# One gather for eight experts, nine whole units, and the overflow branch behind the output

## The chip, the cores and the metric

The kernel runs on one core of one Trainium2 chip. The time is that of the device for one execution, in microseconds. TensorE is PE, with its weight loads as PEld; VectorE is DVE, ScalarE is ACT, GpSimd is POOL, and SyncE (SP) issues nearly all of the DMAs. Three executions of the kernel before took 1276.86, 1276.93 and 1277.24 us; the median is 1276.93.

## The reference

Two transformer blocks over 256 tokens of 1024 values, in fp32. The first has a gated mixer of three branches and a feed-forward layer; it isn't touched. The second has two kinds of attention and, at its end, a layer of 32 experts, to which nearly all of the change belongs:

```python
h2 = _modulate(_rmsnorm(x, g_ffn), shift_ffn, scale_ffn)
group = argmax(softmax(h2 @ w_group))                     # 1 of 4 groups
top_p, top_local = top_k(softmax(expert logits within the group), 2)
weight = group_gate * top_p / sum(top_p)
y[token] = sum over its two experts e of
           weight * ((silu(h2 @ w_gate[e]) * (h2 @ w_up[e])) @ w_down[e])
x = x + gate_ffn * y
out = _rmsnorm(x, g_final)
```

Each expert has w_gate and w_up (1024x512) and w_down (512x1024): 6 MiB in fp32, 192 MiB for all 32.

## The kernel before

**Units.** All weights come as units of 1 MiB (128 partitions x 2048 values), in the order of a plan: 127 units for what stands ahead of the experts, then 192, six for each expert (two each of `eg`, `eu` and `ed`: gate, up and down). `prefetch` (L295) issues a unit's DMA on SP (L302) as soon as one of 18 buffers (`units`) is free and fewer units than a cap wait unconverted. The `units` buffers also hold the converted weights, the hidden values `gy` and a few others, so that the release of any of them can let a DMA start.

**Conversion.** TensorE multiplies in a reduced form of fp32 (fp32r), so each unit is split: ACT rounds it (`hi<-raw`, L221, where all of ACT's operations are recorded), DVE subtracts (`lo<-raw,hi`, L344), and PE multiplies with both (`pe<-hi,xs`, `pe<-lo,xs`; all of PE's matmuls are recorded at L237). `take_unit` (L350) converts two units ahead of the one in use. A *whole* unit (`whole`, L290) isn't split: PE takes it as plain fp32, one pass over `raw` that needs more time per column (each of its matmuls shows as two records). Counted from the first expert unit, units 9, 25, 41, ..., 185 are whole: twelve.

**Order.** The program runs over pairs of experts, p = 0 to 16. In step p stand gate and up of experts 2p and 2p+1 (`gate_up`), in their middle the hidden layer of pair p-1 (`hidden`: `pT<-cst,gy`, silu, `hsz`), and then the downs of pair p-1 (`down`: `pd`); so 12 units a step. Each expert has 32 token slots. `gather(g)` copies tokens into the slots of four experts, by 32 matmuls with a 0/1 matrix `oh` (`pg`), split into high and low part, and eight copies by ACT into `xs` (two buffers, each for four experts). `put_back` brings the results of eight experts back to the tokens: 32 fp32 matmuls (`py<-ws,gy`, 64 records), then additions to `x` on DVE (L1582). It comes after p=4, 8 and 12, for four pairs each; a put_back of three pairs, 12 to 14, comes after p=15, and one of the last pair at the end. When it is done, its `gy` buffers come free.

Such pieces stand in a list `bg`. `pull` takes one piece of it for each half unit, so gathers and put_backs are strewn between the matmuls of the units; `drain` empties the list at once. `post` sets off a step some half units later, and `flush` does all that are due. `st["order"]` = 1 holds the strewn pieces behind the conversion just issued.

**End.** More tokens may choose an expert than it has slots. How many are left over is summed (`full`, L1635), brought to one value by a matmul (`pn`), and turned into a number (`left`, L1639); every engine loads that (L1640) and passes a branch (`tc.If`, L1641). Behind it is a loop over all experts for the tokens left over; with these inputs there are none. After the branch come the last put_back, the sum of squares (`ss<-sq,ones`), `rstd` and the output, written in place of `x` and sent by four DMAs.

Of the kernel before, what the change touches and what calls it, by code (L numbers as in the profile page):

```python
# [213 lines left out]
def block_kernel(ctx: ExitStack, tc: tile.TileContext, A, out):  # L214
# [21 lines left out]
    def mm(*a, **k):  # L236
        last["mm"] = T.matmul(*a, **k).ins  # L237
# [21 lines left out]
    def ps(name="ps"):  # L259
        return psum.tile([P, 512], F32, name=name, tag="ps")  # L260
# [4 lines left out]
    def t256(name, dt=F32, shape=(P, 256)):  # L265
        return tmp.tile(list(shape), dt, name=name, tag="r", bufs=4)
# [7 lines left out]
    def flat(ap):  # L274
        return ap.rearrange("p k t -> p (k t)")

    def over2(r):
        return bc(r[:, None, :], [P, 2, 256])
# [11 lines left out]
    def whole(u):  # L290

        m = u - MOE0
        return m < NU - MOE0 - 4 and m % 16 == 9

    def prefetch(upto=-1):  # L295
        while st["dma"] < NU and ((len(raw) < st["cap"] and live[0] < NS) or st["dma"] <= upto):
# [99 lines left out]
    def post(fn, n=1):  # L396
        due.append((st["step"] + n, fn))
# [15 lines left out]
    def flush():  # L413
        settle(True)
# [18 lines left out]
    def drain():  # L433
        while bg or bg2:
            pull(1000)
# [67 lines left out]
    def rstd_of(acc, mult=1.0):  # L503
        r = t256("rstd")
        act(r, acc[:, :256], AF.Sqrt, bias=epst, scale=mult)
        V.reciprocal(r, r)  # L506
        return r
# [892 lines left out]
    def weights():  # L1400

        V.tensor_tensor(ge, lg[:, :, 0:4], bc(gv[:, :, None], [P, 2, 4]), op=OP.subtract)
        V.tensor_tensor(ge, ge, bc(rk[:, :, None], [P, 2, 4]), op=OP.mult)
        act(ge, ge, AF.Exp)
        V.tensor_tensor(ed, top[:, 1], top[:, 0], op=OP.subtract)
        V.tensor_tensor(ed, ed, rk, op=OP.mult)
        act(ed, ed, AF.Exp)
        V.tensor_tensor(ms, at, end_slot, op=OP.is_lt)
        V.tensor_tensor(jk, pick, bc(ms[:, None], [P, 2, 2, 32]), op=OP.mult)
        V.tensor_reduce(fit, jk, axis=AX.X, op=OP.add)  # L1410
        V.tensor_reduce(gs, ge, axis=AX.X, op=OP.add)
        V.reciprocal(gs, gs)
        V.tensor_scalar(wt[:, 1], ed, 1.0, None, op0=OP.add)
        V.reciprocal(wt[:, 1], wt[:, 1])
        V.tensor_tensor(wt[:, 0], gs, wt[:, 1], op=OP.mult)
        V.tensor_tensor(wt[:, 1], wt[:, 0], ed, op=OP.mult)
        for q in range(1, 4):
            slg.append(rtile(2, 2))
            V.tensor_scalar(slg[q], sl, -256.0 * q, None, op0=OP.add)


    xg, wsel = {}, {}
# [6 lines left out]
        G.memset(t[:, :, :, 64:128].bitcast(F32), 0.0)  # L1429
    for t in hsz:  # L1430
        G.memset(t[:, :, 64:128].bitcast(F32), 0.0)
    ohs = {}

    def gather(g):

        if g % 2 == 0:
            oh = ohs[g // 2] = [pairs.tile([P, 256], F32R, name="oh", tag="oh", bufs=4) for tt in range(2)]
            for tt in range(2):
                t1 = t256("oh1")
                V.tensor_scalar(t1, slot, slg[g // 2][:, 0, tt:tt + 1], None, op0=OP.is_equal)  # L1440
                last["oh"] = V.scalar_tensor_tensor(oh[tt], slot, slg[g // 2][:, 1, tt:tt + 1], t1,
                                                    op0=OP.is_equal, op1=OP.add).ins
            yield
            yield
        oh = [t[:, (g % 2) * 128:(g % 2 + 1) * 128] for t in ohs[g // 2]]
        for k2 in range(4):
            p = ps("pg")
            for kk in range(2):
                k = 2 * k2 + kk
                for i, h in enumerate((hth, htl)):  # L1450
                    c = slice(kk * 256 + i * 128, kk * 256 + (i + 1) * 128)
                    for tt in range(2):
                        mm(p[:, c], h[:, tt, k * 128:(k + 1) * 128], oh[tt],
                           start=kk + i + tt == 0, stop=tt == 1, skip_group_check=True)

            def keep(k2=k2, p=p):
                pv = p.rearrange("p (k i a b r) -> p k i a b r", k=2, i=2, a=2, b=2)
                for kk in range(2):
                    o = xs[g % 2][:, 2 * k2 + kk].rearrange("p a (h i r) -> p a h i r", h=3, i=2)
                    last["xg"] = act(o[:, :, 0:3:2], pv[:, kk].rearrange("p i a b r -> p a b i r"), AF.Copy)  # L1460
            post(keep, 2)
            yield

    def put_weights(g):
# [61 lines left out]
    def hidden(q):  # L1526

        t = gy[q]
        p = ps("pT")
        for f in range(8):  # L1530
            mm(p[:, f * 64:(f + 1) * 64], t[:, f * 128:(f + 1) * 128], fold, start=True, stop=True)
        sg = t256("sgm")
        hs = hsz[q % 2]
        sv = sg.rearrange("p (f e r) -> p f e r", f=4, e=2)
        ho = hs.rearrange("p f (h i r) -> p f h i r", h=3, i=2)

        def product():
# [12 lines left out]
    def down(e, hs):  # L1550
        odd = e % 2 == 1
        if not odd:
            pds[:] = [ps("pd"), ps("pd")]
        for k2 in range(2):
            for ws in take_unit("ed", e, k2):
                rows_times([(pds[n], window(hs[:, 2 * k2 + i], e), 2 * i + n, not odd and k2 + i == 0,
                             odd and k2 + i == 2) for i in range(2) for n in range(2)])(ws)
        if odd:
            y = gy[e // 2]

            def keep(pd=list(pds)):
                for n in range(2):
                    if n and e == NE - 1:
                        V.tensor_copy(y[:, n * 512:(n + 1) * 512], pd[n])
                    else:
                        act(y[:, n * 512:(n + 1) * 512], pd[n], AF.Copy)
            post(keep, 2)
# [37 lines left out]
    for p in range(NE // 2 + 1):  # L1605
        if p < NE // 2:
            gate_up(2 * p)
        if p:
            if p == NE // 2:
                flush()  # L1610
            hs = hidden(p - 1)
            if p == NE // 2:
                flush()
        if p < NE // 2:
            gate_up(2 * p + 1)
            if p % 2 == 0 and p < NE // 2 - 2:
                bg.append(gather(p // 2 + 1))
            if p % 4 == 2:
                bg.append(put_weights(p // 4))
            if p % 2 == 1:  # L1620
                drain()
        if p:
            for e in (2 * p - 2, 2 * p - 1):
                down(e, hs)
            if p % 4 == 0 and p < NE // 2:
                post(lambda p=p: bg.insert(0, put_back([p - 4, p - 3, p - 2, p - 1])), 3)
            elif p == NE // 2 - 1:
                post(lambda p=p: bg.insert(0, put_back([p - 3, p - 2, p - 1])), 3)
# [2 lines left out]
    flush()  # L1631


    full = tmp.tile([P, 1], F32, name="full", tag="full", bufs=1)
    V.tensor_reduce(full, fit, axis=AX.XY, op=OP.add)  # L1635
    pn = ps("pn")
    mm(pn[:1, :1], full, one1[:, 0:1], start=True, stop=True)
    left = tmp.tile([1, 1], mybir.dt.int32, name="left", tag="left", bufs=1)
    V.tensor_scalar(left, pn[:1, :1], -1.0, 512.0, op0=OP.mult, op1=OP.add)  # L1639
    n_left = nc.values_load(left, min_val=0, max_val=512)  # L1640
    with tc.If(n_left > 0):  # L1641
        hx = k8(unit("hx"))
# [66 lines left out]
                                           op0=OP.mult, op1=OP.add)  # L1709
            free(6)  # L1710
        free(2)


    acc = ps("ss")

    zero = tmp.tile([P, 1], F32, name="zero", tag="full", bufs=1)
    ctx.enter_context(tc.issue_after(act(zero, x[:, 0, 0:1], AF.Sqrt, scale=0.0)))
    V.tensor_add(epst, epst, zero)
    back = []
    for _ in put_back([NE // 2 - 1], back.append):  # L1720
        pass
    end = last["mm"]
    for f2, add in enumerate(back):
        add()
        with tc.issue_after(end):
            square_sum(acc, flat(x[:, 2 * f2:2 * f2 + 2]), f2 == 0, f2 == 3)
    r = rstd_of(acc)
    for k2 in range(4):
        for k in (2 * k2, 2 * k2 + 1):
            act(x[:, k], x[:, k], AF.Copy, scale=vec("g_final_2", k))  # L1730
        x2 = x[:, 2 * k2:2 * k2 + 2]
        (G if k2 == 3 else V).tensor_tensor(x2, x2, over2(r), op=OP.mult)  # L1732
        nc.sync.dma_start(out[:, 2 * k2:2 * k2 + 2], x2)


# [19 lines left out]
```

## Time and profile before

| | us |
|---|---|
| median of three executions | 1276.93 |
| the profiled execution | 1279.84 |
| its span, first to last instruction | 1278.0 |
| PE busy in it | 1204.2 (94%) |
| DVE busy | 1034.0 (81%) |
| ACT busy | 796.7 (62%) |
| mean granted TensorE clock | 0.975 |

The span is what the trace shows; the profiled execution is 1.84 us longer, and 2.9 us above the median. Times in the rows count from the start of the span. The expert part runs from about 740 to 1252 us. HBM reads are 338.88 MB in all.

### The profile page before, as it was taken

Reading aid. Unit: us, or ns where it says so; the run is one execution under the profiler, and the core shown is the slowest. Engines: PE = TensorE matmul, PEld = TensorE weight load, DVE = VectorE, ACT = ScalarE, POOL = GpSimd, SP = SyncE. Lnnn points to the kernel's source line nnn. Section 1 sums busy time; section 2 is a strip of 40 time slices with the busy share of each in tenths; the row PEclk is TensorE's granted clock in tenths of the full one; section 3 lists DMA queues with packets and bytes.
Section 4 is the critical chain, followed back from the end, with each engine's and each line's share of the span. In section 5 each row is a group of like instructions: output and inputs, shape, how many; then the busy total and the mean of one; then the engine's idle time right before and its main releaser. Section 6 shows DMA issues by size and latency. Waiting matters only on the chain. (4 is left out here: it accounts for less than half of the span.)

```text
span 1278.0 us, 19089 instructions
## 1 busy us (share of the span) xinstructions
PE 1204.2 (94%) x7588; PEld 1058.0 (83%) x7588; DVE 1034.0 (81%) x1221; ACT 796.7 (62%) x917; POOL 105.3 (8%) x106
## 2 busy tenths in 40 slices
PE   6987999999999999889999999999999999999984
PEld 6985899999999999888888878777877787778763
DVE  6699999968798889666646778986998699869973
ACT  5576645375654444645465379886888688867852
POOL 2559400210000000000000000000000000000000
PEclk9999999999999999999989989999999999999997
DMA  9732257437887988232127059999899989998941
GB/s 365 283 132 99 100 201 276 150 116 285 333 301 295 343 322 322 108 133 99 67 72 291 1 198 415 421 421 387 336 421 421 400 342 421 422 395 334 421 199 35
DMA packets 48622, 341.22 MB, mean 267 GB/s; under 512 B 5392, under 2 KB 5648, under 8 KB 7824
## 3 DMA queue, kind: packets, MB, share of 16 engines
q1 hardware_dynamic: 47664, 337.65, 66.8%
q10 hardware_dynamic: 864, 2.31, 0.5%
q8 instruction: 61, 1.00, 0.3%
q14 instruction: 33, 0.27, 0.1%
HBM read 338.88 MB, written 1.05 MB: 266 GB/s over the span
## 5 line engine op out<-in xcount | busy, mean ns | idle before, releaser
L221 ACT ACTIVATE hi<-raw 128x1024 fp32r<-128x1024 f32 (+1 forms) x388 | 556.8, 1453 | 299.0 <-issue 47.6
L344 DVE TENSOR_TENSOR lo<-raw,hi 128x2048 fp32r<-128x2048 f32 (+1 forms) x182 | 405.1, 2264 | 67.6 <-ACT hi L221 48.9
L323 DVE TENSOR_TENSOR lo<-raw,hi 128x1024 fp32r<-128x1024 f32 x206 | 259.8, 1268 | 75.9 <-ACT hi L221 72.0
L237 PE MATMUL pe<-lo,xs 128*128 128x512 f32 x480 | 135.0, 406 | 5.9 <-DVE lo L344 5.5
L237 PE MATMUL pe<-hi,xs 128*128 128x512 f32 x480 | 137.3, 410 | 1.2 <-ACT xs L221 1.1
L237 PEld LDWEIGHTS pe<-lo,xs 128*128 128x128 f32 x480 | 87.5, 189 | 34.1 <-DVE lo L344 15.9
L237 PEld LDWEIGHTS pe<-hi,xs 128*128 128x128 f32 x480 | 89.9, 191 | 25.7 <-issue 3.3
L640 DVE SCALAR_TENSOR_TENSOR ca<-ch,par,ca 128x246 f32<-128x246 f32 (+25 forms) x180 | 100.8, 588 | 0.9
L237 PE MATMUL pd<-hi,hsz 128*128 128x512 f32 x240 | 68.0, 405 | 3.0 <-DVE hsz L1543 3.0
L237 PE MATMUL pd<-lo,hsz 128*128 128x512 f32 x240 | 67.0, 401 | 2.0 <-DVE lo L344 1.6
L237 PE MATMUL py<-ws,gy 128*128 128x256 f32 x256 | 60.3, 392 | 5.9 <-PEq L1641 5.5
L237 PEld LDWEIGHTS py<-ws,gy 128*128 128x128 f32 x256 | 50.2, 197 | 14.0 <-issue 5.5
L631 POOL TENSOR_TENSOR ca<-ca,tap 128x255 f32<-128x255 f32 (+29 forms) x60 | 57.9, 966 | 33.2 <-ACT tap L221 29.6
L237 PEld LDWEIGHTS pd<-hi,hsz 128*128 128x128 f32 x240 | 45.1, 188 | 15.9 <-issue 5.3
L314 DVE SCALAR_TENSOR_TENSOR raw<-raw,aux 128x1024 f32<-128x1024 f32 x48 | 56.8, 1220 | 0.0
L237 PEld LDWEIGHTS pd<-lo,hsz 128*128 128x128 f32 x240 | 44.4, 189 | 14.9 <-DVE lo L344 5.1
L237 PE MATMUL pgt<-nh,hi 128*128 128x256 f32 x192 | 54.2, 282 | 0.0
L237 PE MATMUL pgt<-nl,hi 128*128 128x256 f32 x192 | 53.9, 281 | 0.0
L237 PE MATMUL pgt<-nh,lo 128*128 128x256 f32 x192 | 53.7, 280 | 0.0
L237 PE MATMUL pfg<-xh,hi 128*128 128x256 f32 x176 | 49.7, 282 | 0.0
L237 PE MATMUL pfg<-xl,hi 128*128 128x256 f32 x176 | 49.5, 281 | 0.0
L237 PE MATMUL pfg<-xh,lo 128*128 128x256 f32 x176 | 49.5, 281 | 0.0
(349 smaller groups left out, 2954.7 us busy)
## 6 DMA issues: line engine op xcount, KB each, us to landing
raw<-in_ws_dram SPq DMA_DIRECT2D x318, 1024.0 KB, 8.7
x<-in_xt_dram SPq DMA_DIRECT2D x4, 256.0 KB, 4.2
raw<-in_ws_dram SPq DMA_DIRECT2D x2, 512.0 KB, 8.1
out_dram<-x SPq DMA_DIRECT2D x4, 256.0 KB, 2.7
aux<-in_sguw_dram ACTq DMA_DIRECT2D x1, 512.0 KB, 9.6
aux<-in_cnt_dram SPq DMA_DIRECT2D x1, 512.0 KB, 12.7
aux<-in_sgub_dram ACTq DMA_DIRECT2D x1, 512.0 KB, 3.9
aux<-in_cvec_dram ACTq DMA_DIRECT2D x1, 512.0 KB, 4.7
```

Source lines behind the costliest of these rows:

```text
L221: ins = S.activation(out, in_, func, **k).ins
L237: last["mm"] = T.matmul(*a, **k).ins
L314: V.scalar_tensor_tensor(r, r, 1.0, cond["c"], op0=OP.mult, op1=OP.mult, accum_out=mod[:, col:col + 1])
L323: st["lo"] = V.tensor_sub(lo, r, hi).ins
L344: st["lo"] = V.tensor_sub(lo[:, c], raw[u][:, c], hi[:, c]).ins
L631: G.tensor_tensor(ca[:, j, d:], ca[:, j, d:], t[:, :256 - d], op=OP.add)
L640: V.scalar_tensor_tensor(ca[:, j, d:], ch[:, j, :256 - d], w(30 - d), ca[:, j, d:], op0=OP.mult, op1=OP.add)
```

## The change

1. `gather(g)` serves eight experts: 32 matmuls of 256 columns into eight `pg` tiles, and sixteen copies into both `xs` buffers. There are four gathers in place of eight. The first stands ahead of the loop, as before; the others are listed at p=3, 7 and 11 instead of at every second p, behind a `drain`, with two pieces pulled for each half unit (`st["bg"] = 2`), and end with a `drain` behind the downs.
2. `whole` takes every twentieth unit: 9, 29, 49, ..., 169, nine in all. Units 57, 105, 153 and 185 among others are split now.
3. At p=16 the list is emptied ahead of the last hidden layer, and the strewn order is given up (`st["order"] = 0`): the put_back of pairs 12 to 14 is written out there.
4. `full`, `pn` and `left` are computed at the start of the expert part (`weights`).
5. The last put_back, the sum of squares, `rstd` and the output (`finish`, to a new buffer `xo`) stand ahead of the branch, and once more in it, for the case of left tokens.

```diff
-        return m < NU - MOE0 - 4 and m % 16 == 9
+        return m < NU - MOE0 - 4 and m % 20 == 9
...
+        V.tensor_reduce(full, fit, axis=AX.XY, op=OP.add)
+        pn = ps("pn")
+        mm(pn[:1, :1], full, one1[:, 0:1], start=True, stop=True)
+        V.tensor_scalar(left, pn[:1, :1], -1.0, 512.0, op0=OP.mult, op1=OP.add)
...
-        for k2 in range(4):
+        yield
+        for k in range(8):
             p = ps("pg")
...
+            for i, h in enumerate((hth, htl)):
+                for tt in range(2):
+                    mm(p[:, i * 256:(i + 1) * 256], h[:, tt, k * 128:(k + 1) * 128], oh[tt],
+                       start=i + tt == 0, stop=tt == 1, skip_group_check=True)
+
+            def keep(k=k, p=p):
+                pv = p.rearrange("p (i g a b r) -> p g a b i r", g=2, i=2, a=2, b=2)
+                for half in range(2):
+                    o = xs[half][:, k].rearrange("p a (h i r) -> p a h i r", h=3, i=2)
+                    last["xg"] = act(o[:, :, 0:3:2], pv[:, half], AF.Copy)
+            post(keep, 1)
             yield
...
         if p:
             if p == NE // 2:
                 flush()
+                drain()
+                flush()
+                st["order"] = 0
             hs = hidden(p - 1)
...
-            if p % 2 == 0 and p < NE // 2 - 2:
-                bg.append(gather(p // 2 + 1))
+            if p % 4 == 3 and p // 4 < 3:
+                drain()
+                bg.append(gather(p // 4 + 1))
+                st["bg"] = 2
             if p % 4 == 2:
                 bg.append(put_weights(p // 4))
-            if p % 2 == 1:
-                drain()
         if p:
             for e in (2 * p - 2, 2 * p - 1):
                 down(e, hs)
+            if st["bg"] == 2:
+                drain()
+                st["bg"] = 1
...
+    def finish(back):
+
+        acc = ps("ss")
+        xo = k8(unit("xo"))
+        for f2, add in enumerate(back):
+            add()
+            with later(last.get("end")):
+                square_sum(acc, flat(x[:, 2 * f2:2 * f2 + 2]), f2 == 0, f2 == 3)
+        r = rstd_of(acc)
+        for k2 in range(4):
+            for k in (2 * k2, 2 * k2 + 1):
+                act(xo[:, k], x[:, k], AF.Copy, scale=vec("g_final_2", k))
+            x2 = xo[:, 2 * k2:2 * k2 + 2]
+            (G if k2 == 3 else V).tensor_tensor(x2, x2, over2(r), op=OP.mult)
+            nc.sync.dma_start(out[:, 2 * k2:2 * k2 + 2], x2)
+        free()
...
+        for _ in put_back([NE // 2 - 1], back.append):
+            pass
+        last["end"] = last["mm"]
+        finish(back)
...
     n_left = nc.values_load(left, min_val=0, max_val=512)
     with tc.If(n_left > 0):
...
+        last["end"] = None
+        finish([lambda: None] * 4)
```

The first place is the first gather, on PE. `pg` are the gather's matmuls, `pe` those of gate and up. Before:

```order
L237 MATMUL pg<-oh,htl 128x128
L237 MATMUL pe<-hi,xs 128x512 x2
L237 MATMUL pg<-oh,hth 128x128 x2
L237 MATMUL pg<-oh,htl 128x128 x2
L237 MATMUL pg<-oh,hth 128x128 x2
L237 MATMUL pg<-oh,htl 128x128 x2
L237 MATMUL pe<-hi,xs 128x512 x5
L237 MATMUL pe<-lo,xs 128x512 x4
L237 MATMUL pe<-hi,xs 128x512
L237 MATMUL pe<-lo,xs 128x512 x4
L237 MATMUL pg<-oh,htl 128x128
L237 MATMUL pg<-oh,hth 128x128 x2
```

And now:

```order
L237 MATMUL pg<-oh,hth 128x256
L237 MATMUL pg<-oh,htl 128x256 x5
L237 MATMUL pn<-one_103,full 1x1
L237 MATMUL pe<-hi,xs 128x512 x4
L237 MATMUL pe<-lo,xs 128x512 x4
L237 MATMUL pe<-hi,xs 128x512 x4
L237 MATMUL pe<-lo,xs 128x512 x4
L237 MATMUL pe<-hi,xs 128x512 x7
```

The `pe` matmuls that stood between the pieces of this gather, and the second gather's pieces after them, are behind it or gone; `pn` has come from the end of the program.

The second place is the first put_back, on PE (`py`), around the units 56 to 58. Before:

```order
L237 MATMUL pe<-hi,xs 128x512 x4
L237 MATMUL py<-ws,gy 128x256 x9
L237 MATMUL pe<-lo,xs 128x512 x4
L237 MATMUL pe<-raw,xs 128x512 x4
L237 MATMUL pe<-hi,xs 128x512 x4
L237 MATMUL py<-ws,gy 128x256 x18
L237 MATMUL pe<-lo,xs 128x512 x4
L237 MATMUL py<-ws,gy 128x256 x5
L237 MATMUL pe<-hi,xs 128x512 x4
L237 MATMUL pe<-lo,xs 128x512 x4
```

And now:

```order
L237 MATMUL pe<-hi,xs 128x512 x4
L237 MATMUL py<-ws,gy 128x256 x9
L237 MATMUL pe<-lo,xs 128x512 x4
L237 MATMUL pe<-hi,xs 128x512 x4
L237 MATMUL pe<-lo,xs 128x512 x4
L237 MATMUL pe<-hi,xs 128x512 x4
L237 MATMUL py<-ws,gy 128x256 x18
L237 MATMUL pe<-lo,xs 128x512 x4
L237 MATMUL py<-ws,gy 128x256 x5
L237 MATMUL pe<-hi,xs 128x512 x4
L237 MATMUL pe<-lo,xs 128x512 x4
```

The whole unit (`pe<-raw`) has become a pair of `hi` and `lo`; the pieces of put_back stand at the same places.

The third place is the end, on PE: the last downs (`pd`), the put_back of pairs 12 to 14, and the output. Before:

```order
L237 MATMUL pT<-cst,gy 128x64 x4
L237 MATMUL pd<-lo,hsz 128x512 x4
L237 MATMUL py<-ws,gy 128x256 x4
L237 MATMUL pd<-hi,hsz 128x512 x4
L237 MATMUL pd<-lo,hsz 128x512 x4
L237 MATMUL py<-ws,gy 128x256 x12
L237 MATMUL pd<-hi,hsz 128x512 x4
L237 MATMUL pd<-lo,hsz 128x512 x4
L237 MATMUL py<-ws,gy 128x256 x6
L237 MATMUL pd<-hi,hsz 128x512 x4
L237 MATMUL pd<-lo,hsz 128x512 x4
L237 MATMUL pd<-hi,hsz 128x512 x4
```

And now:

```order
L237 MATMUL pd<-lo,hsz 128x512 x4
L237 MATMUL py<-ws,gy 128x256 x16
L237 MATMUL pd<-hi,hsz 128x512 x4
L237 MATMUL pd<-lo,hsz 128x512 x4
L237 MATMUL pd<-hi,hsz 128x512 x4
L237 MATMUL pd<-lo,hsz 128x512 x4
L237 MATMUL pd<-hi,hsz 128x512 x4
L237 MATMUL pd<-lo,hsz 128x512 x4
L237 MATMUL pd<-hi,hsz 128x512 x4
L237 MATMUL pd<-lo,hsz 128x512 x4
L237 MATMUL py<-ws,gy 128x256 x8
L237 MATMUL ss<-sq,ones 128x256 x8
```

The pieces of `py` that alternated with the last four units stand ahead of them in one row, and the last pair's `py` and `ss`, which before came behind the branch, follow the last `pd` directly.

## Rows read from the trace of the kernel before

**Rows 1.** Busy time of the engines, from the page: engine, us (share of the span), instructions.

```profile
PE 1204.2 (94%) x7588; PEld 1058.0 (83%) x7588; DVE 1034.0 (81%) x1221; ACT 796.7 (62%) x917; POOL 105.3 (8%) x106
```

**Rows 2.** Windows in the expert part: from:to and length in us, busy time of PE, PEld, DVE, ACT and POOL (with instructions), granted TensorE clock, DMA share, GB/s.

```profile
740.00:756.00 16.00, 14.80 (x64) 11.99 (x64) 10.30 (x6) 10.72 (x10) 0.00 (x0) 0.88 0.35 130
...
852.00:868.00 16.00, 15.60 (x82) 12.60 (x81) 14.82 (x10) 13.01 (x10) 0.00 (x0) 1.00 1.01 422
...
884.00:900.00 16.00, 16.00 (x68) 12.71 (x67) 7.93 (x9) 5.48 (x3) 0.00 (x0) 1.00 0.62 240
900.00:916.00 16.00, 16.00 (x78) 13.23 (x77) 15.81 (x12) 13.87 (x12) 0.00 (x0) 1.00 0.98 366
...
740.00:1252.00 512.00, 499.36 (x2299) 391.32 (x2298) 433.32 (x286) 389.25 (x341) 0.00 (x0) 1.00 0.91 371
```

**Rows 3.** Waits of SP, which issues the DMAs: line waiting, what it waited for, us in total, times, longest.

```profile
SPq L302 <- PE py L237: 36.3, 3, 12.1
...
SPq L1750 <- DMA out_dram<-x: 2.7, 1, 2.7
```

**Rows 4.** Timeline of the start of the expert part: start and length in us, engine, line, operation, names, shapes, count [idle before, released by].

```profile
739.25 1.16 PE L237 MATMUL pe<-hi,xs 128*128 128x512 f32 x2
...
741.81 2.37 PE L237 MATMUL pe<-hi,xs 128*128 128x512 f32 x5
...
744.27 2.29 DVE L344 TENSOR_TENSOR lo<-raw,hi 128x2048 fp32r<-128x2048 f32 x1 [4.15 <-PE pe L237]
...
745.15 1.92 ACT L221 ACTIVATE hi<-raw 128x2048 fp32r<-128x2048 f32 x1 [4.23 <-PE pe L237]
...
749.42 2.81 SPq L302 DMA_DIRECT2D raw<-in_ws_dram  x2
```

**Rows 5.** A window in which PE ran `po` matmuls of 256 columns in fp32r back to back: from:to and length, busy us (instructions), granted clock, DMA share, GB/s.

```profile
705.00:713.00 8.00, 8.00 (x69) 1.00 0.01 2
```

**Rows 6.** The same columns for the `pg` matmuls (128 columns) of the gather before the first put_back and of the very first gather.

```profile
867.40:870.05 2.65, 2.62 (x24) 1.00 1.01 417
735.00:739.00 4.00, 4.00 (x20) 0.50 0.00 0
```

**Rows 7.** Groups of instructions between 725 and 1252 us: line, engine, operation, names, shapes, count | busy us, mean ns | idle before, by releaser.

```profile
L344 DVE TENSOR_TENSOR lo<-raw,hi 128x2048 fp32r<-128x2048 f32 x178 | 400.3, 2288 | 67.0 <-ACT hi L221 48.2 <-issue 14.6 <-PE pe L237 4.2
L221 ACT ACTIVATE hi<-raw 128x2048 fp32r<-128x2048 f32 x178 | 336.8, 1918 | 81.5 <-PE pe L237 41.5 <-PE py L237 16.8 <-PE pd L237 13.9
...
L221 ACT ACTIVATE xs<-pg 128x256 fp32r<-128x256 f32 x64 | 20.1, 400 | 6.4 <-PE pg L237 6.0
```

**Rows 8.** Timeline of the first put_back, columns as in rows 4.

```profile
872.91 1.10 PE L237 MATMUL pd<-hi,hsz 128*128 128x512 f32 x4
...
873.85 1.10 PE L237 MATMUL pd<-lo,hsz 128*128 128x512 f32 x4
...
878.11 4.05 PE L237 MATMUL py<-ws,gy 128*128 128x256 f32 x18
...
882.93 3.60 PE L237 MATMUL pe<-raw,xs 128*128 128x512 f32 x8
...
885.96 1.50 PE L237 MATMUL pe<-hi,xs 128*128 128x512 f32 x4
...
887.29 7.93 PE L237 MATMUL py<-ws,gy 128*128 128x256 f32 x36
888.50 2.29 DVE L344 TENSOR_TENSOR lo<-raw,hi 128x2048 fp32r<-128x2048 f32 x1 [3.50 <-ACT hi L221]
...
896.25 2.29 DVE L344 TENSOR_TENSOR lo<-raw,hi 128x2048 fp32r<-128x2048 f32 x1 [4.42 <-issue]
...
898.35 3.79 ACT L221 ACTIVATE hi<-raw 128x2048 fp32r<-128x2048 f32 x2 [5.61 <-PE py L237]
```

**Rows 9.** Timeline of the last downs, columns as in rows 4.

```profile
1229.86 1.18 PE L237 MATMUL pd<-lo,hsz 128*128 128x512 f32 x4
...
1236.54 1.17 PE L237 MATMUL pd<-hi,hsz 128*128 128x512 f32 x4 [3.05 <-DVE hsz L1543]
...
1238.48 5.34 PE L237 MATMUL py<-ws,gy 128*128 128x256 f32 x24
...
1250.92 1.10 PE L237 MATMUL pd<-lo,hsz 128*128 128x512 f32 x4
```

**Rows 10.** Timeline of the end, columns as in rows 4.

```profile
1251.83 0.60 ACT L221 ACTIVATE gy<-pd 128x512 f32<-128x512 f32 x1 [15.99 <-PE pd L237]
...
1252.07 0.69 DVE L1564 COPY gy<-pd 128x512 f32<-128x512 f32 x1 [2.87 <-PE pd L237]
...
1257.62 6.24 PE L237 MATMUL py<-ws,gy 128*128 128x256 f32 x16 [5.47 <-PEq L1641]
...
1263.70 3.62 PE L237 MATMUL ss<-sq,ones 128*128 128x256 f32 x16
...
1267.39 0.46 ACT L221 ACTIVATE rstd<-ss,epst 128x256 f32<-128x256 f32 x1
```

**Rows 11.** Windows of the end, columns as in rows 2.

```profile
1256.00:1258.00 2.00, 0.38 (x1) 0.41 (x2) 0.00 (x0) 0.00 (x0) 0.00 (x0) 0.50 0.00 0
...
1262.00:1264.00 2.00, 2.00 (x9) 1.71 (x8) 1.25 (x4) 0.92 (x3) 0.00 (x0) 0.80 0.00 0
```

**Rows 12.** The DMAs of `raw` between 740 and 1000 us.

```profile
DMA to landing us min/median/max: 4.8/10.3/14.4
```

More of the change, by code (lines that the diff above doesn't have):

```diff
@@ L1419, in weights @@
             V.tensor_scalar(slg[q], sl, -256.0 * q, None, op0=OP.add)
+        V.tensor_reduce(full, fit, axis=AX.XY, op=OP.add)
+        pn = ps("pn")
+        mm(pn[:1, :1], full, one1[:, 0:1], start=True, stop=True)
+        V.tensor_scalar(left, pn[:1, :1], -1.0, 512.0, op0=OP.mult, op1=OP.add)
+    full = tmp.tile([P, 1], F32, name="full", tag="fl", bufs=1)
+    left = tmp.tile([1, 1], mybir.dt.int32, name="left", tag="left", bufs=1)
     xg, wsel = {}, {}
@@ L1431, in block_kernel @@
         G.memset(t[:, :, 64:128].bitcast(F32), 0.0)
-    ohs = {}
     def gather(g):
[L1436 to L1445, printed above, removed]
-        for k2 in range(4):
-            p = ps("pg")
[L1448 to L1461, printed above, removed]
@@ new lines, in gather @@
+        oh = [pairs.tile([P, 256], F32R, name="oh", tag="oh", bufs=4) for tt in range(2)]
+        for tt in range(2):
+            t1 = t256("oh1")
+            V.tensor_scalar(t1, slot, slg[g][:, 0, tt:tt + 1], None, op0=OP.is_equal)
+            last["oh"] = V.scalar_tensor_tensor(oh[tt], slot, slg[g][:, 1, tt:tt + 1], t1,
+                                                op0=OP.is_equal, op1=OP.add).ins
+        yield
+        for k in range(8):
+            p = ps("pg")
+            for i, h in enumerate((hth, htl)):
+                for tt in range(2):
+                    mm(p[:, i * 256:(i + 1) * 256], h[:, tt, k * 128:(k + 1) * 128], oh[tt],
[6 more added lines that the diff above has]
+            post(keep, 1)
@@ L1631, in block_kernel @@
     flush()
[L1634 to L1639, printed above, removed]
+    def finish(back):
[13 more added lines that the diff above has]
+        free()
+    zero = tmp.tile([P, 1], F32, name="zero", tag="full", bufs=1)
+    with tc.issue_after(act(zero, x[:, 0, 0:1], AF.Sqrt, scale=0.0)):
+        V.tensor_add(epst, epst, zero)
+        back = []
+        for _ in put_back([NE // 2 - 1], back.append):
+            pass
+        last["end"] = last["mm"]
+        finish(back)
     n_left = nc.values_load(left, min_val=0, max_val=512)
@@ L1711, in block_kernel @@
         free(2)
[L1714 to L1733, printed above, removed]
+        last["end"] = None
+        finish([lambda: None] * 4)
 def kernel(**inputs):
```

## The prediction

> **What bounds the kernel now.** I read the page first, then the windows of the expert part, then the waits of the DMA queue, and last the timelines at four places. By the page TensorE is busy almost everywhere, VectorE next [rows 1], which points to TensorE. The windows of the expert part (740 to 1252 us, 40% of the span) say otherwise: in an undisturbed stretch the DMA moves 422 GB/s at a share of 1.01, the most that any window shows, while PE, DVE and ACT all still have a little room [rows 2]. There the stream of weights is the bound: a unit is 1 MiB, 1.0486 MB / 421 GB/s = 2.49 us, the 48 units of eight experts 119.5 us. Only where that stream breaks is there something to win without moving fewer bytes, and no byte is saved here. It breaks at the first gather (130 GB/s), in and after the first put_back (240, then 366 GB/s) and after the last byte, when PE works alone [rows 2]. Those windows lose (421 - 240)/421 x 16 = 6.9 us and (421 - 366)/421 x 16 = 2.1 us, so 9 us. The waits of the DMA queue name the put_back itself, all three of them alike: three waits for the last `py` matmul, 36.3 us in all, since a unit buffer freed by put_back is the next one to fill [rows 3].
>
> **The change part by part.** The sum is made against the profiled execution, 1279.84 us (span 1278.0), which lies 2.9 us above the median of 1276.93; the answer is moved by that at the end.
>
> *Start of the expert part.* Before, the stream stands still until 749.42; then the queue issues again [rows 4]. What it needs is the conversion of the first units, and this is held up behind matmuls: PE puts two and then five `pe` matmuls between the pieces of gather(0), and the second gather follows at once; DVE's `lo` at 744.27 had waited 4.15 us, ACT's `hi` at 745.15 4.23 us. After, 32 matmuls of 256 columns stand in one row, and the second gather's work is in them. At the full clock 256 columns take 8.00/69 = 0.116 us [rows 5], 128 columns 2.62/24 = 0.109 us [rows 6]; at half clock 128 columns take 0.20 us (4.00/20 [rows 6]). So two gathers before are 64 x 0.109 = 7.0 us at full clock, one of eight experts 32 x 0.116 = 3.7 us; here, at a granted clock of 0.50, I take 32 x 0.23 = 7.4 us in place of 32 x 0.20 plus the later 32 x 0.11 = 9.9 us. With the `pe` matmuls out of the way I put the restart 3 us earlier (749.4 to 746.4); bounds 0 and -5 (749.42 - 744.27 is the whole stretch from `lo` to issue). The `full`, `pn` and `left` steps moved here are three instructions on a column or a single value, beside longer ones on each engine: nothing, at worst 0.3 us.
>
> *The gathers in the loop.* Total PE work falls by 4 x 7.0 - 4 x 3.7 = 13 us, ACT's copies stay 64 of 400 ns [rows 7]. PE isn't the bound in full stretches, so this is worth nothing there. What counts is where they stand. Before, a gather's 3.5 us ended right in front of the first put_back: `pg` until 870.05 [rows 6], `py` from 878.11 [rows 8]. After, at p=3, 7 and 11, they stand among the downs, some 12 units ahead of it, and 16 copies come to ACT close together: 16 x 0.40 = 6.4 us. A unit every 2.49 us leaves ACT 2.49 - 1.92 = 0.57 us a unit for other things and DVE 2.49 - 2.29 = 0.20 us [rows 7]. The block thus sets ACT back by 6.4 less the room of the two units under way, 5.3 us. On the 12 units to put_back it makes up 12 x 0.29 = 3.5 us (half of the 0.57, since its other copies take the rest), and +1.8 us arrives there as lag, each time. If the units already converted hide it all, 0; if nothing is made up, +5.
>
> *The three put_backs.* Each is 32 fp32 matmuls, 64 records, unchanged: 4.05 and 7.93 us at the first two of its three places [rows 8]. Units 57, 105 and 153, whole units, stand in the middle of them. A whole unit's matmuls begin at 882.93 and the next group at 885.96, and that group is slow too (887.29 is next, 1.33 us): 4.36 us for what takes three groups of four, 3 x 0.94 = 2.82 us, as a pair (such groups start 0.94 us apart, 872.91 and 873.85 [rows 8]): -1.5 us each. The unit then needs a conversion, 2.29 us on DVE and 1.92 on ACT; DVE is only busy 7.93 of 16 us there [rows 2] and waits 3.5 and 4.4 us, so it lies beside. The gather just ahead is gone: -2.6 us each, the length of its 24 records [rows 6]. With the lag of +1.8 this is -2.3 us each, three times -6.9 us. Bounds for one: +3.5 (lag 5, and of the two savings only the pair's 1.5) and -8.5 (the break is all but gone).
>
> Three more conversions add 3 x 2.29 = 6.9 us to DVE: 433.32 us over the whole part [rows 2] become 440.2, or 110 us for eight experts against the stream's 119.5. That hides them; if not, 6.9/3 = +2.3 us per put_back, inside the bound.
>
> *The drain.* When the last weights have come, PE still has four units and the put_back of pairs 12 to 14. Before, 8 `py` records run, PE waits 3.05 us for `hsz`, then pieces of `py` and units alternate until 1252.02 [rows 9]. After, 8 `py` matmuls go in front, where PE waits for weights, and 16 behind e=29's last unit, over the wait for `hsz`. From 1231.04, the end of that unit: 0.5 us for the `gy` copy, 16 x 0.44 = 7.0 us of `py` (24 records in 5.34 us are 0.22 each, two records a matmul), four units of 1.85 us = 7.4 us: 1231.04 + 14.9 = 1245.9. Unit 185, now a pair, adds a conversion that DVE must do before: 1 us of its 2.29 counts. 1246.9 against 1252.0: -5. Bounds 0 (the early `py` delays the units by as much) and -6.
>
> *The tail.* Before, ACT's copy ends at 1252.43 and DVE's at 1252.76, and PE starts `py` at 1257.62 after 5.47 us at its branch [rows 10]; the granted clock is 0.50 when it starts after this rest, and 0.80 on average six microseconds later [rows 11], so most of these matmuls run at the lower level of 1.2 GHz. After, nothing stands between: `py` at 1252.87 in those times, -4.75 us, and PE has rested under 1 us, so eight matmuls take 8 x 0.44 = 3.5 us in place of 6.1 (1257.62 to 1263.70): rstd follows 3.7 us behind the last one, as it does now (1267.39), -2.5 us. The branch moves behind the output: its register load and jump on SP lie beside the 2.7 us that the last output takes to land [rows 3]; PE, which stood 5.47 us at it, will be done with `ss` some 10 us before the end (now 1267.39 to 1278.0). I put +0.5 us there. Tail -6.75.
>
> The Trainium skill ("Runtime: NRT & Kernel Launch", Instruction fetch mechanics) says that a taken branch to code outside the window held on the engine stops it for a fetch. The 5.47 us row of PE [rows 10] agrees, and no row shows such a stop on another engine. By that rule alone SP, ACT and DVE would pay at the moved branch too, and the output's second copy in the branch makes the jump longer; the rival D below carries it.
>
> Sum: -3 - 6.9 - 5 - 6.75 = -21.65; 1279.84 - 21.65 = 1258.2 profiled, and 2.9 less, 1255.3, in the median. I say 1255.
>
> **The rivals.** A, the middle gives nothing: the copies' lag at each put_back eats what pair and gather give, and the restart comes no earlier. For it: ACT's wait for `py` in put_back (5.61 us [rows 8]) is the real limit and stays. Against: the two savings are on PE, in a place where PE has no idle time. Left are drain and tail, -11.75: about 1265 in the median. B, the stalls nearly vanish because PE arrives at put_back ahead: 3 x -8.5 in place of -6.9, 18.6 us less: 1237; against it, the freed buffer still waits for the last `py`. C, slower: the gather block in the downs, 3.7 us of PE and 6.4 us of ACT at one spot, starves the conversions, the stream stops there as it does at put_back (9 us each, three times +27), while put_back keeps its own 9: 1276.9 + 27 - 14.75 = 1289. It decides if ACT's block delays the conversions beyond what the buffered units cover, from about four units, 10 us, on; for it speaks ACT's room of only 0.57 us a unit; against it, that ACT copies the same number of tiles as before and that a unit takes 10.3 us from issue to landing [rows 12], so that some four (10.3/2.49) are on their way when it begins. D, the branch's price reappears at the end on SP or ACT: it stood at 5.47 us on PE; if other engines pay it behind the output, that is 4.75 us more: 1260.
>
> **How the numbers follow.** Forecast 0.53, A 0.19, B 0.10, C 0.08, D 0.10. The forecast's own range is 1249 to 1261. For 8 in 10 I take 1244 to 1268: it holds the forecast, A and D, and leaves out C and most of B. What a measurement of this kernel can tell from no change is about 0.2%, 2.6 us. Faster is the forecast, A, B and D, less a few parts where the bounds of the middle add to the bad side: 0.88; same 0.04; slower 0.08.
>
> **What would show each step.** In the profile after: no wait of PE for its branch ahead of the last `py`, and a granted clock of 1.00 through `ss`; the first break of the stream, 130 GB/s in its window now, shorter by some 3 us; in the windows around each put_back more than 240 and 366 GB/s, 9 us of loss down to about 6.5; `py` x16 directly behind e=29's last `pd` and 5 us less from last landing to last `pd`. Wrong would be: a new break of the stream at p=3, 7, 11 (rival C), put_back windows as before (A), or engines that stay at the branch after the last output landed (D).

## The result, and the profile after

The change makes the kernel slower: 1285.64 us in the median of six executions (1281.55 to 1288.50), against 1277.09 for six of the kernel before (1273.86 to 1281.04). The ratio is 1.0059, with a 95% interval of 1.0042 to 1.0076. Forecast were 1255 us and a range of 1244 to 1268. Single executions lay up to 4 us on either side of their median in these twelve, more than the three of before had shown.

The profiled execution of the changed kernel took 1285.96 us, its span 1283.9. Cut at four marks that the timeline and the DMA rows of the weights show, the two spans differ like this (us):

| stretch | before | after | difference |
|---|---|---|---|
| start to the first `pg` | 734.5 | 742.1 | +7.6 |
| first `pg` to the next weights issued | 14.9 | 11.5 | -3.4 |
| from there to the last weights issued | 468.0 | 478.6 | +10.6 |
| last weights issued to the last `pd` | 34.6 | 32.0 | -2.6 |
| last `pd` to the end | 26.0 | 19.7 | -6.3 |
| span | 1278.0 | 1283.9 | +5.9 |

The first and the last mark are the start of the first `pg` and the end of the last `pd` in the timeline. The two between are the first and the last start in the row of the DMAs of `raw` from 740 us on (count, duration in ns, first and last start), here of the kernel before:

```profile
L302 SPq DMA_DIRECT2D raw<-in_ws_dram x181: 327/328/805, 749.4 to 1217.5; - x181
```

and of the changed kernel:

```profile
L302 SPq DMA_DIRECT2D raw<-in_ws_dram x181: 327/328/813, 753.6 to 1232.2; - x181
```

Two things stand out. The first stretch holds no instruction that the change touches, and still is 7.6 us longer. And the stream of weights, where 6.9 us were to be won, takes 10.6 us more. The windows of the changed kernel show where (columns as in [rows 2]):

```profile
836.00:852.00 16.00, 9.34 (x40) 7.67 (x40) 11.98 (x9) 9.83 (x14) 0.00 (x0) 0.68 1.01 421
852.00:868.00 16.00, 16.00 (x84) 13.54 (x84) 11.60 (x7) 14.92 (x19) 0.00 (x0) 1.00 0.98 369
...
900.00:916.00 16.00, 16.00 (x79) 13.45 (x79) 15.26 (x14) 11.29 (x9) 0.00 (x0) 1.00 0.80 306
...
964.00:980.00 16.00, 11.05 (x34) 7.39 (x33) 13.91 (x12) 8.88 (x8) 0.00 (x0) 0.79 1.01 421
980.00:996.00 16.00, 16.00 (x88) 13.29 (x87) 8.15 (x4) 14.27 (x23) 0.00 (x0) 1.00 0.82 314
...
1092.00:1108.00 16.00, 9.57 (x40) 7.07 (x39) 14.45 (x10) 11.08 (x10) 0.00 (x0) 0.90 1.01 420
1108.00:1124.00 16.00, 15.42 (x76) 13.23 (x77) 8.57 (x7) 12.75 (x24) 0.00 (x0) 0.89 0.82 304
...
1156.00:1172.00 16.00, 16.00 (x82) 13.93 (x80) 10.48 (x10) 7.04 (x4) 0.00 (x0) 1.00 0.63 241
```

In [rows 2], PE is busy for 15 to 16 us of each such window and the clock is 1.00 in all but the first. Now three windows, 836, 964 and 1092, have PE busy for 9 to 11 us only, at a granted clock of 0.68 to 0.90, and behind each of them comes a window in which the stream falls to 369, 314 and 304 GB/s: breaks where there were none. The kernel before has, at two of these places:

```profile
980.00:996.00 16.00, 15.60 (x82) 12.59 (x81) 14.82 (x10) 13.01 (x10) 0.00 (x0) 1.00 1.01 420
...
1108.00:1124.00 16.00, 15.60 (x82) 12.60 (x81) 14.82 (x10) 13.01 (x10) 0.00 (x0) 1.00 1.01 421
```

The new breaks are the gathers at p=3, 7 and 11. The timeline of the first of them:

```profile
835.26 1.20 PE L237 MATMUL pe<-lo,xs 128*128 128x512 f32 x4 [0.40 <-DVE lo L344]
835.46 6.69 DVE L344 TENSOR_TENSOR lo<-raw,hi 128x2048 fp32r<-128x2048 f32 x3
...
842.07 0.61 DVE L1444 TENSOR_SCALAR oh<-cst,rt 128x256 f32<-128x256 f32 x2
...
842.59 0.87 DVE L1445 SCALAR_TENSOR_TENSOR oh<-cst,rt,oh 128x256 fp32r<-128x256 f32 x2
...
843.12 0.58 PE L237 MATMUL pg<-oh,hth 128*128 128x256 f32 x1 [6.66 <-DVE oh L1445]
...
843.50 1.91 PE L237 MATMUL pd<-hi,hsz 128*128 128x512 f32 x4
```

PE stands still for 6.66 us in front of the first `pg`. What it waits for is `oh`, two short steps on DVE for each of two matrices, and these stand behind three conversions in DVE's queue (6.69 us). The downs (`pd`) that PE could have done meanwhile stand behind the `pg`. At p=7 two conversions stand there, and the wait is 4.46 us; at p=11 it is 6.66 us again. PE's waits over the whole execution (what it waited for: us, times, longest) have a row that the kernel before doesn't have:

```profile
PE pg L237 <- DVE oh L1445: 17.8, 3, 6.7
```

The standstill also slows what follows. In windows of 2 us (same columns) the granted clock goes from 1.00 to 0.50 while PE stands still, which is 1.2 in place of 2.4 GHz, stays there for the first 5 us of new work, and the four `pd` at 843.50 take 1.91 us, where [rows 8] has 1.10:

```profile
836.00:838.00 2.00, 0.46 (x2) 0.02 (x1) 2.00 (x2) 1.42 (x2) 0.00 (x0) 1.00 1.00 418
838.00:840.00 2.00, 0.00 (x0) 0.00 (x0) 2.00 (x2) 2.00 (x2) 0.00 (x0) 0.60 1.01 422
840.00:842.00 2.00, 0.00 (x0) 0.00 (x0) 2.00 (x1) 0.22 (x1) 0.00 (x0) 0.50 1.02 426
...
846.00:848.00 2.00, 2.00 (x8) 1.74 (x7) 1.80 (x1) 0.17 (x1) 0.00 (x0) 0.50 1.01 422
848.00:850.00 2.00, 2.00 (x10) 1.62 (x10) 0.22 (x1) 1.75 (x1) 0.00 (x0) 0.84 1.02 426
```

The DMA runs on at 418 to 426 GB/s through all this, into buffers that are free; only some 10 us after PE's new start, when PE's delay has kept buffers from being given back, does it break. SP's waits (columns as in [rows 3]) for buffers that the downs give back show it, before:

```profile
SPq L302 <- PE pd L237: 36.6, 27, 2.9
```

and after:

```profile
SPq L302 <- PE pd L237: 64.5, 27, 6.8
```

The tail is near its forecast, the drain gives half of its own. The rows that answer to [rows 9] and [rows 10]:

```profile
1247.90 8.86 PE L237 MATMUL py<-ws,gy 128*128 128x256 f32 x32 [1.77 <-ACT gy L221]
...
1264.26 0.69 DVE L1563 COPY gy<-pd 128x512 f32<-128x512 f32 x1 [6.08 <-PE pd L237]
...
1264.67 3.72 PE L237 MATMUL py<-ws,gy 128*128 128x256 f32 x16 [0.45 <-ACT gy L221]
...
1272.56 0.47 ACT L221 ACTIVATE rstd<-ss,epst 128x256 f32<-128x256 f32 x1 [0.82 <-PE ss L237]
```

The last `py` follows the last `pd` after 0.45 us in place of 5.47, and `rstd` starts 7.9 us behind it in place of 9.8.

### The profile page after: what moved, and what is told of

It reads as the page before. It is cut to its first block, busy times and chain, and to the rows that moved or that the text cites. A ratio compares the mean times of both kernels' runs of the same rounds, so it can differ in the third digit from the quotient of the medians.

```text
span 1283.9 us, 18826 instructions
## 1 busy us (share of the span) xinstructions
PE 1194.3 (93%) x7460; PEld 1052.7 (82%) x7460; DVE 1045.1 (81%) x1224; ACT 801.9 (62%) x920; POOL 103.9 (8%) x106
## 5 line engine op out<-in xcount | busy, mean ns | idle before, releaser
L221 ACT ACTIVATE hi<-raw 128x1024 fp32r<-128x1024 f32 (+1 forms) x391 | 562.5, 1456 | 316.6 <-issue 51.9
L344 DVE TENSOR_TENSOR lo<-raw,hi 128x2048 fp32r<-128x2048 f32 (+1 forms) x185 | 412.0, 2264 | 66.0 <-ACT hi L221 55.9
L237 PE MATMUL pe<-hi,xs 128*128 128x512 f32 x488 | 134.0, 400 | 0.1
L237 PE MATMUL pd<-hi,hsz 128*128 128x512 f32 x244 | 71.3, 413 | 3.9 <-DVE hsz L1542 3.9
L237 PE MATMUL pd<-lo,hsz 128*128 128x512 f32 x244 | 70.6, 411 | 2.8 <-DVE lo L344 2.2
L237 PEld LDWEIGHTS py<-ws,gy 128*128 128x128 f32 x256 | 49.6, 194 | 10.6 <-ACT gy L221 3.1
```

Of the source, the lines that this page charges most:

```text
L344: st["lo"] = V.tensor_sub(lo[:, c], raw[u][:, c], hi[:, c]).ins
```

## The experiments

Each time stands beside that of the kernel before on the same chip, which was 1277.53, 1280.80 or 1278.96 us in the median; so kernels measured on different chips are compared by their ratios. In brackets behind a ratio stands its 95% interval.

### The 32 bytes (e1, e2, e8)

The first stretch has the same instructions in the same order on every engine. What differs is where its data lie: `full` got a place of its own (tag "fl"), and everything allocated behind the `tmp` tiles lies 32 bytes further on, among it the halves `hi` and `lo` of the first 127 units (but not `oh`, which the next expectation names too and which lies ahead of `tmp`). The kernel before, with nothing but this:

```diff
-    zero = tmp.tile([P, 1], F32, name="zero", tag="full", bufs=1)
+    zero = tmp.tile([P, 1], F32, name="zero", tag="fl", bufs=1)
```

> The kernel before, with every instruction as it was; only the tile of `zero` at the end gets a place of its own, so that everything placed behind the `tmp` tiles (the halves `hi` and `lo` of the first 127 units, `oh`, `xs`, `hsz` among them) lies 32 bytes further on, as it does in the changed kernel. Theory P (placement): the 7 us that the changed kernel's profile shows before the experts begin come from these 32 bytes; this kernel is then 5 to 8 us slower than before, its first `pg` starts near 741 and not 734.5, and `pgt` matmuls follow each other at 0.120 us in place of 0.117. Rival C (chance of the execution or of the clock): the time is within 2 us of before and `pgt` at 0.117.

Measured: 1280.36 us (ten executions) against 1277.53, ratio 1.0028 (1.0011 to 1.0044): slower, by half of what was expected. And the changed kernel without it:

```diff
-    full = tmp.tile([P, 1], F32, name="full", tag="fl", bufs=1)
+    full = tmp.tile([P, 1], F32, name="full", tag="full", bufs=1)
```

> The changed kernel with the tile `full` back in the place that it shares with `zero`, so that all tiles of the part ahead of the experts lie where they lay before. Theory P: 7 us faster than the changed kernel, about 1277, equal to before within 2 us, since the rest of the change gives -1.2 by its profile. Rival C: it stays at 1284 to 1286.

Measured: 1281.23 us against 1277.53, ratio 1.0039 (1.0023 to 1.0056), between the two expectations: by the ratios the bytes would explain 2.6 us of the loss, and 5 us are left for the rest of the change. The intervals of the two kernels overlap, so that the bytes cost something is shown by e1 and not by this pair. To see whether the place within 64 bytes counts, the third moved the same data by 64:

```diff
-    zero = tmp.tile([P, 1], F32, name="zero", tag="full", bufs=1)
+    zero = tmp.tile([P, 16], F32, name="zero", tag="fl", bufs=1)[:, 0:1]
```

> The kernel before, every instruction as it was, with what lies behind the `tmp` tiles moved by 64 bytes in place of 32. If what counts is where `hi` and `lo` lie within 64 bytes: as before, 1277 within 1.5 us, `lo<-raw,hi` of 128x1024 at 1294 ns and `pgt` at 0.117 to 0.118 us. If any move costs (or the first run with 32 was chance): 1280 and 1320 ns, or no pattern.

Measured: 1282.53 us against 1280.80, ratio 1.0022 (1.0000 to 1.0044). By the time alone that is hardly told from no change, but its conversions are slow as well, and that sinks the idea of a place within 64 bytes. The row of the conversion in four kernels between 160 and 280 us (count, busy us, mean ns, idle before), first of the kernel before:

```profile
L323 DVE TENSOR_TENSOR lo<-raw,hi 128x1024 fp32r<-128x1024 f32 x40 | 51.8, 1294 | 3.3 <-ACT hi L221 3.0
```

moved by 32 bytes, e1:

```profile
L323 DVE TENSOR_TENSOR lo<-raw,hi 128x1024 fp32r<-128x1024 f32 x40 | 52.8, 1321 | 4.7 <-ACT hi L221 4.3
```

and by 64, e8:

```profile
L323 DVE TENSOR_TENSOR lo<-raw,hi 128x1024 fp32r<-128x1024 f32 x40 | 52.7, 1318 | 4.8 <-ACT hi L221 4.5
```

The changed kernel has 1320 there, e2 1295. So the same DVE operation takes 2% more with its data elsewhere, on every profile with moved data. The first `pg` came at 742.1, 738.0, 736.3 and 739.5 us in the changed kernel, e1, e3 and e8 (moved, mean 739.0), and between 732.4 and 737.9 in the ten profiles with data in the old place (mean 735.3): 3.6 us on average, but a single execution scatters by as much. So the place may account for about half of the 7.6 us in the first table; the other half is within the scatter. Which operand's place matters was not tried.

### The early `oh` (e3, e5)

The matrices `oh` are computed ahead of `gate_up(2p+1)`, four units before the gather, with the same instructions (the one empty step that was left behind them goes, too):

```diff
+            if p % 4 == 3 and p // 4 < 3:
+                post(lambda g=p // 4 + 1: prepare(g), 1)
             gate_up(2 * p + 1)
...
-        oh = [pairs.tile([P, 256], F32R, name="oh", tag="oh", bufs=4) for tt in range(2)]
...
+        oh = ohs[g]
```

> The changed kernel (with the 32 bytes) whose 0/1 matrices `oh` are computed four units earlier, ahead of the gate and up matmuls of the step, and no longer right in front of the gather. Theory G: PE's wait of 6.7 us for `oh` at each of three gathers, with the lower clock behind it, is what cost the middle; without it the waits are under 1 us, the clock in these stretches 1.00, and the kernel 10 to 17 us faster than the changed one (1268 to 1275). Rival A (ACT's sixteen copies are the cost, as the prediction had it): the wait goes but the time falls by under 4 us.

Measured: 1263.55 us against 1277.53, ratio 0.9900 (0.9884 to 0.9917): by the ratios 20 us faster than the changed kernel, more than expected, though the 32 bytes are still in it. The row of the wait for `oh` is gone. Without the bytes:

> The run with the early `oh` (e3), and the 32 bytes taken back. If both causes are right and add up: e3's 1263.6 less the 3 to 4 us that the 32 bytes cost, about 1260, 17 us faster than before; waits for `oh` under 1 us, `lo<-raw,hi` of 128x1024 near 1295 ns. If the bytes play no part here: 1263 to 1264.

Measured: 1262.52 us against 1280.80, ratio 0.9864 (0.9837 to 0.9891). By the ratio 17 us faster than before, as expected; in microseconds only 1 us below e3, on another chip. In its windows the gather's stretch is whole again, and the first put_back loses (421 - 354 + 421 - 401)/421 x 16 = 3.3 us and not the 9 of the kernel before:

```profile
852.00:868.00 16.00, 15.94 (x61) 11.01 (x60) 14.29 (x9) 13.08 (x11) 0.00 (x0) 1.00 1.02 423
...
884.00:900.00 16.00, 16.00 (x80) 13.63 (x80) 11.57 (x11) 9.14 (x7) 0.00 (x0) 1.00 0.89 354
900.00:916.00 16.00, 16.00 (x69) 11.79 (x67) 14.97 (x9) 13.75 (x11) 0.00 (x0) 1.00 1.01 401
...
1012.00:1028.00 16.00, 16.00 (x74) 12.35 (x73) 10.09 (x11) 6.26 (x6) 0.00 (x0) 1.00 0.69 265
1028.00:1044.00 16.00, 16.00 (x78) 13.24 (x77) 15.07 (x7) 15.43 (x12) 0.00 (x0) 1.00 0.98 377
```

The second put_back still loses (421 - 265 + 421 - 377)/421 x 16 = 7.6 us, as in the kernel before (256 and 382 GB/s, 7.8 us); why the first alone gains stays open. The stretches of all profiles, as in the table above:

| | to `pg` | to weights | stream | to last `pd` | to end | span |
|---|---|---|---|---|---|---|
| before | 734.5 | 14.9 | 468.0 | 34.6 | 26.0 | 1278.0 |
| after | 742.1 | 11.5 | 478.6 | 32.0 | 19.7 | 1283.9 |
| e1, before + 32 bytes | 738.0 | 11.0 | 466.7 | 37.3 | 26.3 | 1279.2 |
| e2, after - 32 bytes | 734.7 | 11.6 | 482.3 | 31.9 | 19.6 | 1280.0 |
| e3, early `oh` | 736.3 | 11.5 | 461.6 | 31.9 | 19.7 | 1261.1 |
| e5, both | 736.3 | 11.6 | 462.6 | 30.4 | 19.7 | 1260.5 |
| e6, e5, p=16 of before | 734.1 | 11.5 | 462.5 | 35.0 | 20.2 | 1263.4 |
| e7, e5, twelve whole | 735.5 | 11.5 | 463.4 | 30.6 | 20.3 | 1261.3 |
| e9, e5, gathers of before | 737.9 | 14.2 | 468.7 | 32.0 | 19.9 | 1272.8 |
| e10, e5, end of before | 736.3 | 10.7 | 462.5 | 30.4 | 25.0 | 1264.9 |
| e4, before + tail | 732.4 | 14.6 | 468.0 | 36.2 | 20.1 | 1271.3 |
| e8, before + 64 bytes | 739.5 | 11.3 | 467.5 | 34.6 | 25.7 | 1278.4 |
| e11, before, no empty steps | 737.3 | 11.1 | 480.7 | 37.3 | 26.0 | 1292.4 |
| e12, e5, six whole | 734.4 | 11.5 | 463.9 | 30.4 | 19.9 | 1260.1 |

Between e2 and e5 lies the early `oh` alone: 482.3 - 462.6 = 19.7 us of stream, for waits of 18.4 us in e2 and 0 in e5. The wait and the half clock behind it go together in these runs; their shares were not told apart.

### The wait in the kernel before (e11)

Was it the wide gather, or the distance between `oh` and its reader? The kernel before had two empty steps there:

```diff
                                                     op0=OP.is_equal, op1=OP.add).ins
-            yield
-            yield
         oh = [t[:, (g % 2) * 128:(g % 2 + 1) * 128] for t in ohs[g // 2]]
```

> The kernel before, without the two empty steps between the computing of `oh` and the first `pg` matmul; the gathers stay at 128 columns and four experts. If the lost distance is the cause, and not the width of 256 columns or the block of sixteen copies: PE waits some 5 to 7 us for `oh` at three of the gathers, the clock falls to 0.50 there, and the kernel is 10 to 18 us slower than before. If it takes the change's gather to bring out the wait: within 2 us of before.

Measured: 1289.99 us against 1278.96, ratio 1.0087 (1.0059 to 1.0114). PE's waits:

```profile
PE pg L237 <- DVE oh L1441: 13.0, 3, 4.8
```

The windows around the first of the three waits (columns as in [rows 2]):

```profile
800.00:816.00 16.00, 11.21 (x36) 7.44 (x35) 13.14 (x12) 8.95 (x8) 0.00 (x0) 0.82 1.01 422
816.00:832.00 16.00, 16.00 (x91) 13.80 (x90) 12.86 (x13) 12.85 (x15) 0.00 (x0) 0.96 0.89 334
```

The waits are a little shorter than expected (two conversions stand ahead of the first, not three); the granted clock falls to 0.50 at each, and the stream is 480.7 - 468.0 = 12.7 us longer. Two lines less make the old kernel at least as slow as the changed one. The width of 256 columns and the block of copies are not needed for the loss.

### The parts one by one (e4, e6, e7, e9, e10)

e4 has the tail of the change alone on the kernel before (`weights`, `finish` ahead of the branch; the diff of the change without its `gather`, `whole` and p=16 parts).

> The kernel before with the tail of the change alone: `full`, `pn`, `left` at the start of the expert part, the output ahead of the branch; gather, whole units, the put_back of pairs 12 to 14 and all places as before. By the change's own profile the tail gives 6.3 us: 6 us faster than before, about 1271; up to 3 more if the start gains from `pn`, too. Rival D (the branch's price comes back at the end): 2 us or nothing.

Measured: 1274.89 us against 1277.53, ratio 0.9982 (0.9966 to 0.9999): less than half of the expected gain. Its last stretch is 5.9 us shorter, but the one ahead of it is 1.6 us longer, and the median moved by 2.6 us; where the other 2 us went, single profiles don't tell. The same part taken out of e5, `full`, `pn`, `left`, branch and output as in the kernel before:

> The run e5 with the end of the kernel before: `full`, `pn`, `left` and the branch ahead of the last put_back and the output. By the profiles the tail is worth 6 us (26.0 us from the last `pd` to the end before, 19.7 after): 6 us slower than e5, with PE's wait of 5 us at the branch back and the clock at 0.50. If e4's median tells the truth (2.6 us faster than before with the tail alone): 2 to 3 us slower.

Measured: 1267.06 us against 1278.96, ratio 0.9904 (0.9869 to 0.9940), against 0.9864 for e5: the tail is worth about 0.0040 x 1277 = 5 us there. The two intervals overlap a little, but the last stretch is 25.0 us and not 19.7, and the wait is back:

```profile
PE py L237 <- PEq L1647: 5.3, 1, 5.3
```

The put_back of pairs 12 to 14 back at its old place:

```diff
             if p == NE // 2:
                 flush()
-                drain()
-                flush()
-                st["order"] = 0
```

> The run e5 without the change at p=16: the put_back of pairs 12 to 14 is strewn among the last four units as in the kernel before. By e3's profile, in which the stretch from the last landing to the last `pd` is 17.7 us and not 20.9, this part is worth 3 us: 3 us slower than e5, and the stretch back to 20 or 21 us. If the part is worth nothing (PE has the same matmuls to do behind the last unit, in whatever order): within 1 us of e5.

Measured: 1264.94 us on e5's chip, 2.4 us slower than e5; the stretch is 35.0 us and not 30.4. Twelve whole units:

```diff
-        return m < NU - MOE0 - 4 and m % 20 == 9
+        return m < NU - MOE0 - 4 and m % 16 == 9
```

> The run e5 with the twelve whole units of before (every sixteenth; 57, 105 and 153 inside the put_backs). By the prediction's term (1.5 us of PE at each put_back): 4 to 5 us slower than e5. If the term is nothing because the stream recovers it: within 1 us of e5; if the three conversions saved on DVE count for more: faster than e5 by up to 3 us.

Measured: 1264.07 us, 1.5 us slower than e5 and not 4 to 5, inside what these four executions each scatter; the stream is 0.8 us longer. And the gathers of the kernel before in e5:

```diff
-            if p % 4 == 3 and p // 4 < 3:
-                drain()
-                bg.append(gather(p // 4 + 1))
-                st["bg"] = 2
+            if p % 2 == 0 and p < NE // 2 - 2:
+                bg.append(gather(p // 2 + 1))
```

> The run e5 with the gathers of the kernel before: eight, for four experts each, of 128 columns, every second step, with `oh` two half units ahead as before; all else of the change stays. By the prediction (2.6 us of PE less in front of each put_back, 1.8 us of lag more, and half of the start's 3 us) the gather for eight is worth some 4 us: 4 us slower than e5, the put_back windows losing 7 to 8 us and not 3.3. If the gather for eight is worth nothing once its `oh` is early: within 1 us of e5.

Measured: 1272.22 us against 1278.96, ratio 0.9944 (0.9928 to 0.9960), against e5's 0.9864: the gather for eight, with its `oh` early, is worth 0.0080 x 1277 = 10 us, more than twice the expectation. In the profiles 2.6 us of it lie at the start, 6.1 in the stream, 1.6 behind it.

### Six whole units (e12)

> The run e5 with six whole units in place of nine (9, 39, 69, 99, 129, 159). If each whole unit costs PE more than its conversion costs DVE, as from twelve to nine (1.5 us for three): 1 to 1.5 us faster. If DVE's room is used up by then: the same or up to 2 us slower, with fuller DVE windows and a stream below 421 GB/s between the put_backs.

Measured (`m % 30 == 9`): 1261.11 us against 1278.96, ratio 0.9853 (0.9823 to 0.9884). It is the fastest version that was run, but not told apart from e5; both beat the kernel before and the changed one.

## Why the prediction was wrong

The sign and the size of the result come from one term that the sum didn't have. The step that failed is "the gathers in the loop". It counted what the gather takes away on PE and what the sixteen copies put on ACT; it put the cost where it looked, on ACT, at +1.8 us for each put_back. It never asked what the first `pg` waits for. The diff had it: two `yield`s behind `oh` became one, and `st["bg"] = 2` pulls two pieces for each half unit, so `oh` and its first reader came out side by side, `oh` at the tail of DVE's queue and `pg` in the middle of PE's. DVE's queue was known to be long there: conversions take 2.29 us of each 2.49 [rows 7]. Three of them in front of `oh` are 6.9 us; PE came 1.0 us after the first had begun, and the first `oh` took another 1.0 us, which gives the wait that was measured, 6.66 us. In place of a gain of 6.9 us, the stream took 10.6 us more, and computing `oh` four units earlier took 20 us off the time.

Point by point:

- The bound (the stream of weights, and its breaks) was read rightly, though 422 GB/s is not the most that a window shows (424 and 426 in others). A wait on PE of 18 us that the stream doesn't see while it lasts still cost 19.7 us of stream.
- Rival C had the sign and the place, a break of the stream at p=3, 7 and 11, but another mechanism (ACT's block starving the conversions) and too high a price, 27 us. With `oh` early the block does no such harm (e3, e5).
- The gather for eight: forecast 0.8 us for each put_back and 3 at the start, some 5 us. Measured with `oh` early: 10 us by the ratios. The gain at put_back was nearly all at the first one; whether a lag of 1.8 us on ACT took it away at the others was not tried.
- The start: -3 forecast, -3.4 measured. But e1 and e8, with the old instructions, have 11.0 and 11.3 us there, too. The size is right, the cause is not shown.
- The whole units: 4.5 us forecast, 1.5 us measured, within the scatter.
- The drain: -5 forecast; -2.6 in the changed kernel, and worth 2.4 us of the time and 4.6 of the stretch by e6. PE waits 1.77 us for the `gy` copy, not 0.5, and the 32 `py` records take 8.86 us, not 7.0.
- The tail: -6.75 forecast, -6.3 in the profile, 5 us by e10. Rival D, the branch's price again at the end, didn't come: SP's wait at the moved branch is 1.6 us, beside the output's landing, and PE, which stops there for 3.48 us, has no more work (rows in the last section).
- Rival A (the middle gives nothing) and B fell with e5: the middle gives 5.4 us of stream.

With the wait and the bytes out, the sum of -21.65 stands against -17 us measured for e5 by its ratio. That they come so near is in part chance: the gather gave twice its term, the whole units a third of theirs, and drain and tail less than forecast.

## What to carry to other kernels

When a piece of work moves, look up what its first instruction waits for, on which engine that is computed, and what is queued ahead of it there: the wait is that queue, here three conversions, however short the producer itself. So a producer should go further ahead of its reader than that queue is long. Tried were two half units (the kernel before) and four units (e3, e5), both without a wait, and none (the changed kernel and e11); two empty steps were worth 11 us in the kernel before. And a time that differs ahead of the first changed instruction belongs to placement or chance: it should be looked for before the change is blamed.

## What the runs showed that was not expected

Moving operands by 32 or by 64 bytes, in a program with the same instructions, made DVE's subtraction of 128x1024 take 1318 to 1321 ns in place of 1294, and the back-to-back `pgt` matmuls (256 columns, in the part ahead of the experts) start 0.119 to 0.120 us apart on average in place of 0.117 to 0.118. The whole kernel became 0.28% slower (0.11 to 0.44) and 0.22% (0.00 to 0.44). Why the old place is the better one stays open.

The moved branch costs SP 1.6 us, where PE stood 5.47 us at the old one [rows 10] and 5.3 us in e10 (what waits, for what: us, times, longest):

```profile
SPq L1668 <- SPq L1668: 1.6, 1, 1.6
```

PE's own record of the branch (its queue of weight loads; duration in ns, start) is 3.86 us long before, so it is the larger part of those 5.47 us:

```profile
L1641 PEldq COMPARE_BRANCH  x1: 3862/3862/3862, 1253.4 to 1253.4; - x1
```

and nearly as long after, where PE has nothing left to do and the output is still to come, so that nothing waits for it:

```profile
L1668 PEldq COMPARE_BRANCH  x1: 3475/3475/3475, 1272.0 to 1272.0; - x1
```

The branch records of the other four engines take 0.05 to 0.08 us in both kernels. So the branch didn't become cheaper; it was moved to where it costs nothing.

The Trainium skill ("Runtime: NRT & Kernel Launch", Instruction fetch mechanics) says that a taken branch stops an engine for a fetch when its target lies outside the pages that the engine holds. PE's records agree with such a stop; what sets its length, and whether SP's 1.6 us are one too, no run here shows.
